# Weight sums and splits of a seven-product pair, emitted in pieces between the running pair's combinations

## The chip, the cores and the metric

One core of a Trainium2 chip runs the whole program in one launch. The metric is the device time of that launch in microseconds (us); less is better. In the profile the engines are PE (TensorE, the matmul engine), PEld (its weight loads), DVE (VectorE), ACT (ScalarE), POOL (GpSimd) and SP (SyncE, which here only issues transfers).

## The reference, cut to what matters

The program computes two layers of a token mixer followed by a gated MLP, in float32. The change is in the MLP of layer 0, which has 512 latent and 256 context tokens (768 columns, kept with paddings as 772), a model width of 1024 and a hidden width of 2816:

```python
u = h @ w_up                                   # 1024 -> 2 x 2816
u = up[:, :-2] * conv_w[0] + up[:, 1:-1] * conv_w[1] + up[:, 2:] * conv_w[2] + conv_b
a, g = jnp.split(u, 2, axis=-1)
return (jax.nn.silu(g) * a) @ w_down
```

## The kernel before

**Three matmuls for one.** An operand is held as a rounded part `h` and a remainder `l = x - h` (a "split": a cast on ACT and a subtraction on DVE). A product is then weight-high by data-high, weight-high by data-low and weight-low by data-high.

**Pairs.** The hidden width is 22 tiles of 128. "Pair j" is tile j of the value half and tile j of the gate half: 256 columns of `w_up`. Pairs 0 to 2 are computed plainly (`up_std`, line 2041). Pairs 3 to 21 use Strassen's scheme with Winograd's sums: the 2x2 blocks are (two halves of the depth) by (value, gate) on the weights, and (two halves of the depth) by (two halves of the 772 columns) on the data. Seven block products take the place of eight. Each is 4 depth tiles x 3 matmuls = 12 matmuls of 386 columns, so a pair is 84 matmuls.

**Weights of a pair** (`job7`, line 1958). Four transfers on SP's queue fill two `raw` tiles. POOL makes four sums of 128x512, q1 to q4 (called S1 to S4 as product operands). ACT and DVE then split the block X11 (from `raw`), the sums, and the second `raw` tile (which holds X12 and X22): five casts and five subtractions. X11 and two of the sums go into four 776-wide slots `ua, ub, la, lb`; the other two sums into `h14, l14`; the second raw tile into `hb, lob`, all 1024 wide. There are 44 slots of the narrow kind (`NSLAB`), of which the split data of the seven products hold 28, and 13 of the wide kind (`N_WIDE`).

**Products and combinations of a pair** (`up7`, line 2062). The four accumulators a0, a1 (value) and g0, g1 (gate) are PSUM banks; odd pairs use `msc` and `dbl0`, even pairs `dbl1` and `sgl` (`sets7`, line 2010), so that two pairs can be under way. In program order: X11 into a0, copied by ACT to t1; S1 into g0, copied by ACT to t5; S2 into a1, added by DVE; an addition on POOL; S3 into g1, added by DVE, and a copy by ACT; X12 into a0; X22 into g0; the gate's additions and its convolution (`conv7`, line 2023: a POOL memset, ACT, and DVE twice or four times); S4 into a1; the value's additions, its convolution, and `gated` (line 2035: SiLU on ACT, a product on POOL, a store).

**What sets the order.** The program emits instructions in an order of its own, and a list scheduler then builds each engine's queue from a simulated timeline: an engine takes the instruction that was emitted first among those whose inputs and slots are ready at that simulated moment. On the chip each queue is worked off in that order, whatever has become ready in the meantime. (In the attention parts PE's order is written by hand; in this stage it is the scheduler's too.) `run_steps` (line 507) emits the weight job of the next pair before the products of the running one (`ahead_by` is 1 here), so all sums and splits of pair j+1 are emitted ahead of every product and combination of pair j. The job of pair 3 is emitted before the first half of plain pair 2.

Of the kernel before, what the change touches and what calls it, by code (L numbers as in the profile page):

```python
# [9 lines left out]
F32R = mybir.dt.float32r  # L10
# [4 lines left out]
ALU = mybir.AluOpType  # L15
# [195 lines left out]
def trunk_kernel(ctx: ExitStack, tc: tile.TileContext, a, out, dbg=None):  # L211
# [3 lines left out]
    V, A, G, SP = (Engine(e, n, est) for e, n in ((nc.vector, "V"), (nc.scalar, "A"), (nc.gpsimd, "G"), (nc.sync, "SP")))  # L215
# [8 lines left out]
    def slab(dt=F32, w=SW, name="sl"):  # L224
        return slabs.tile([128, w], dt, tag="s", name=name)
# [12 lines left out]
    def wide(dt=F32, name="w"):  # L238
        return wides.tile([128, 1024], dt, tag="w", name=name)
# [324 lines left out]
    def rows(w, r0, nk, c0, n):  # L564
        return w[r0:r0 + 128 * nk, c0:c0 + n].rearrange("(k p) n -> p k n", p=128)
# [373 lines left out]
    def layer(l):  # L939
# [792 lines left out]
        tiles = (4, 2, 2, 1)  # L1732
# [152 lines left out]
        def yk(n, k):  # L1885
            hi, lo = s["y"][n][k // 2]
            c = slice(HH * (k % 2), HH * (k % 2) + HH)
            return hi[:, c], lo[:, c]
# [63 lines left out]
        def products7(bank, w, n):  # L1952
            for k in range(4):
                (wh, wl), (yh, yl) = w[k], yk(n, k)
                for i, (w_, m_) in enumerate(((wh, yh), (wh, yl), (wl, yh))):
                    mm(bank, w_, m_, start=k == 0 and i == 0, stop=k == 3 and i == 2)

        def job7(j):

            def load():
                if j == N_STD:
                    for r in (wad, whi, wlo, wst):
                        r.back()
                    tab.clear()
                raw = []
                for half in range(2):
                    t = wide(name="raw")
                    for m, c0 in enumerate((128 * j, FF + 128 * j)):  # L1970
                        SP.dma_start(out=t.rearrange("p (k m n) -> p k m n", k=4, m=2)[:, :, m, :],
                                     in_=rows(w_up, 512 * half, 4, c0, 128))
                    raw.append(t)

                def cut(t):
                    return t.rearrange("p (k n) -> p k n", n=128)

                def tiles(h, l_, c=0, st=128):
                    return [(h[:, c + st * k:c + st * k + 128], l_[:, c + st * k:c + st * k + 128]) for k in range(4)]

                def split(src, h, l_):
                    A.copy(h, src)
                    V.tensor_tensor(l_, src, h.bitcast(F32), op=ALU.subtract)
                xa, xb = (t.rearrange("p (k m n) -> p k m n", k=4, m=2) for t in raw)
                s14, s23 = wide(name="s14"), wide(name="s23")
                q1, q4, q2, q3 = (cut(t[:, c:c + 512]) for t in (s14, s23) for c in (0, 512))

                ua, ub, la, lb = (slab(F32R, name=n) for n in ("ua", "ub", "la", "lb"))
                split(xa[:, :, 0, :], cut(ua[:, 0:512]), cut(la[:, 0:512]))
                G.tensor_tensor(q1, xa[:, :, 1, :], xb[:, :, 1, :], op=ALU.add)  # L1990
                G.tensor_tensor(q2, q1, xa[:, :, 0, :], op=ALU.subtract)
                G.tensor_tensor(q4, xb[:, :, 0, :], q2, op=ALU.subtract)
                G.tensor_tensor(q3, xa[:, :, 0, :], xa[:, :, 1, :], op=ALU.subtract)
                del xa, raw[0]
                h14, l14 = wide(F32R, "h14"), wide(F32R, "l14")
                split(s14[:, :], h14[:, :], l14[:, :])
                hb, lb2 = wide(F32R, "hb"), wide(F32R, "lob")
                split(raw[0][:, :], hb[:, :], lb2[:, :])
                del xb, raw[0]
                split(s23[:, 0:256], ua[:, 512:768], la[:, 512:768])  # L2000
                split(s23[:, 256:1024], ub[:, 0:768], lb[:, 0:768])
                x23 = [(h[:, c:c + 128], l_[:, c:c + 128]) for h, l_, c in
                       [(ua, la, 512), (ua, la, 640)] + [(ub, lb, 128 * k) for k in range(6)]]
                return ({"X11": tiles(ua, la), "X12": tiles(hb, lb2, 0, 256), "X22": tiles(hb, lb2, 128, 256),
                         "S1": tiles(h14, l14), "S4": tiles(h14, l14, 512), "S2": x23[0:4], "S3": x23[4:8]},)
            return load


        sgl2, msc2 = tuple(sgl), tuple(msc)
# [5 lines left out]
        def halves(t, *cols):  # L2015


            if isinstance(t, tuple):
                return [[x[:, 0:HH]] + [u[:, c + HH * i:c + HH * i + HH] for u, c in cols] for i, x in enumerate(t)]
            return [[t.rearrange("p (h n) -> p h n", h=2)[:, :, 0:HH]] +  # L2020
                    [u[:, c:c + HW].rearrange("p (h n) -> p h n", h=2) for u, c in cols]]

        def conv7(m_tile, bank):

            t = slab(name="cv")
            w0, w1, w2 = (cwT[l][:, 44 * i + m_tile:44 * i + m_tile + 1] for i in range(3))
            G.memset(t[:, 0:HW + 2:HW + 1], 0.0)
            for p, x in halves(bank, (t, 1)):
                A.activation(x, p, func=AF.Identity, scale=w1, bias=vecT[l][:, 64 + m_tile:65 + m_tile])
            for c, w in ((2, w0), (0, w2)):  # L2030
                for p, x in halves(bank, (t, c)):
                    V.scalar_tensor_tensor(x, in0=p, scalar=w, in1=x, op0=ALU.mult, op1=ALU.add)
            return t

        def gated(j, ta, tg):
            x = slice(1, 1 + XW)
            s["silu_f"] = A.activation(tg[:, x], tg[:, x], func=AF.Silu)
            G.tensor_tensor(ta[:, x], ta[:, x], tg[:, x], op=ALU.mult)
            G.dma_start(out=adram[j], in_=ta[:, x])

        def up_std(j, half):

            def fn(hi, lo):
                bk = [x for t in sets7[j] for x in banks(t)]
                order = [(k, m) for k in range(4) for m in range(2)] if j + half == 0 else \
                    [(k, m) for m in range(2) for k in range(4)]
                for k, m in order:
                    c = 256 * k + 128 * m
                    ys = [yk(f"Y{half + 1}{g + 1}", k) for g in range(2)]
                    for i, (w_, v) in enumerate(((hi, 0), (hi, 1), (lo, 0))):  # L2050
                        for g in range(2):
                            mm(bk[2 * m + g], w_[:, c:c + 128], ys[g][v], start=half == 0 and k == 0 and i == 0,
                               stop=half == 1 and k == 3 and i == 2)
                    if half == 1 and k == 3:
                        if m == 0:
                            s["ta"] = conv7(j, sets7[j][0])
                        else:
                            gated(j, s.pop("ta"), conv7(KF + j, sets7[j][1]))
                    yield
            return fn  # L2060

        def up7(j):


            def fn(w):
                if j == N_STD:
                    s["y"].pop("Y12")
                bv, bg = sets7[j]
                (a0, a1), (g0, g1) = banks(bv), banks(bg)
                va, vb = slab(name="pa"), slab(name="pb")  # L2070
                t1, t5, t7, u2 = va[:, 0:HH], va[:, HH:HW], vb[:, 0:HH], vb[:, HH:HW]
                products7(a0, w["X11"], "Y11")
                A.copy(t1, a0)
                products7(g0, w["S1"], "T1")
                A.copy(t5, g0)
                products7(a1, w["S2"], "T2")
                V.tensor_tensor(u2, a1, t1, op=ALU.add)
                G.tensor_tensor(t5, t5, u2, op=ALU.add)
                products7(g1, w["S3"], "T3")
                V.tensor_tensor(t7, g1, u2, op=ALU.add)  # L2080
                A.copy(u2, t5)
                products7(a0, w["X12"], "Y21")
                products7(g0, w["X22"], "T4")
                for p, x in halves(bg, (vb, 0)):
                    V.tensor_tensor(p, p, x, op=ALU.add)
                tg = conv7(KF + j, bg)
                products7(a1, w["S4"], "Y22")
                for p, x in halves(bv, (va, 0)):
                    V.tensor_tensor(p, p, x, op=ALU.add)
                gated(j, conv7(j, bv), tg)  # L2090
            return fn
# [246 lines left out]
```

## Time and profile before

| | |
|---|---|
| time, median of 3 runs | 1627.78 us |
| the three runs | 1625.57 to 1628.17 us |
| the profiled execution | 1625.49 us, with a span of 1623.7 us |
| granted TensorE clock, mean of the span | 0.993 |
| busy share of the span | PE 97%, PEld 81%, DVE 65%, ACT 43%, POOL 26% |

The span runs from the first to the last recorded instruction; the 1.8 us outside it are start and end. Times inside are counted from the span's start. Layer 0's seven-product pairs lie at about 455 to 755 us. In a row of a timeline the bracket at the end is the idle time of that engine just before the instruction, and what ended it.

### The profile page before, as it was taken

How to read it: one execution, taken by the hardware profiler on the slowest of the kernel's cores; microseconds unless marked ns; L12 is line 12 of the kernel's file. 1: busy time of each engine (PE TensorE's matmuls, PEld its weight loads, DVE VectorE, ACT ScalarE, POOL GpSimd, SP SyncE). 2: the span in 40 equal slices, each digit the busy share in tenths (PEclk: the TensorE clock that was granted, in tenths of full speed). 3: DMA queues.
4: the chain of work that ended last, by engine and by line, in shares of the span. 5: the costliest groups of instructions: out<-in, count | busy, mean ns of one | idle time of the engine just before them, and what ended most of it. 6: DMA issues, size and time to landing. Idle time of an engine off the chain costs nothing. (4 is left out here: it accounts for less than half of the span.)

```text
span 1623.7 us, 24874 instructions
## 1 busy us (share of the span) xinstructions
PE 1571.5 (97%) x9431; PEld 1317.8 (81%) x9431; DVE 1054.4 (65%) x1860; ACT 706.2 (43%) x1321; POOL 426.1 (26%) x510
## 2 busy tenths in 40 slices
PE   7999999998999999999999999999999999999998
PEld 4777778876999999999888866778776788888886
DVE  6576476875878888887542373957776554545455
ACT  4364354564645544545321242555574432423331
POOL 1105044534356465662000221122202100100000
PEclk9999999999999999999999999999999999999999
DMA  9943342208122323337751555123222233333322
GB/s 317 262 144 117 118 155 71 82 11 246 52 84 84 107 84 96 107 92 237 263 188 52 184 156 134 41 79 120 87 68 88 79 106 98 97 91 91 104 91 78
DMA packets 215411, 193.30 MB, mean 119 GB/s; under 512 B 32648, under 2 KB 185747, under 8 KB 215292
## 3 DMA queue, kind: packets, MB, share of 16 engines
q1 hardware_dynamic: 211036, 174.25, 36.3%
q0 software_dynamic: 4256, 17.47, 2.9%
q8 instruction: 74, 1.21, 0.3%
q14 instruction: 45, 0.37, 0.1%
HBM read 172.51 MB, written 19.18 MB: 118 GB/s over the span
## 5 line engine op out<-in xcount | busy, mean ns | idle before, releaser
L160 ACT CAST whi<-wst 128x1024 fp32r<-128x1024 f32 (+3 forms) x164 | 161.3, 985 | 315.3 <-PE dbl L401 169.3
L160 DVE TENSOR_TENSOR wlo<-wst,whi 128x1024 fp32r<-128x1024 f32 (+1 forms) x139 | 171.5, 1235 | 169.0 <-ACT whi L160 167.3
L160 POOL TENSOR_TENSOR cv<-cv 128x770 f32<-128x770 f32 (+1 forms) x44 | 73.5, 1670 | 382.7 <-ACT cv L160 364.5
L401 PE MATMUL sgl<-hhi,whi 128*128 128x512 f32 (+1 forms) x344 | 132.0, 384 | 2.6 <-ACT cv L160 1.6
L401 PE MATMUL sgl<-hhi,wlo 128*128 128x512 f32 (+1 forms) x344 | 125.8, 366 | 0.0
L401 PE MATMUL sgl<-hlo,whi 128*128 128x512 f32 (+1 forms) x344 | 125.6, 365 | 0.0
L401 PE MATMUL dbl<-alo,whi 128*128 128x512 f32 x346 | 104.9, 358 | 0.0
L401 PE MATMUL dbl<-ahi,whi 128*128 128x512 f32 x346 | 104.9, 358 | 0.0
L401 PE MATMUL dbl<-ahi,wlo 128*128 128x512 f32 x346 | 104.8, 357 | 0.0
L160 DVE SCALAR_TENSOR_TENSOR cv<-dbl,cwT,cv 128x511 f32<-128x511 f32 (+1 forms) x106 | 91.3, 862 | 7.9 <-ACT cv L160 6.8
L401 PE MATMUL dbl<-hhi,wlo 128*128 128x512 f32 x240 | 94.6, 394 | 0.0
L401 PE MATMUL dbl<-hlo,whi 128*128 128x512 f32 x240 | 94.0, 392 | 0.0
L401 PE MATMUL dbl<-hhi,whi 128*128 128x512 f32 x240 | 93.2, 394 | 0.0
L160 DVE SCALAR_TENSOR_TENSOR x<-dbl,modT,x 128x256 f32<-128x256 f32 (+1 forms) x75 | 48.1, 662 | 64.7 <-PE dbl L401 64.2
L160 POOL TENSOR_TENSOR wlo<-wst,whi 128x640 fp32r<-128x640 f32 (+2 forms) x25 | 42.8, 1712 | 157.4 <-ACT whi L160 157.4
L401 PEld LDWEIGHTS sgl<-hhi,whi 128*128 128x128 f32 x344 | 64.8, 188 | 23.0 <-issue 9.1
L401 PEld LDWEIGHTS sgl<-hhi,wlo 128*128 128x128 f32 x344 | 64.8, 188 | 11.3
L401 PEld LDWEIGHTS sgl<-hlo,whi 128*128 128x128 f32 x344 | 64.8, 189 | 10.8 <-issue 0.5
L160 DVE SCALAR_TENSOR_TENSOR x<-sgl,modT,x 128x256 f32<-128x256 f32 (+1 forms) x70 | 44.5, 648 | 44.5 <-PE sgl L401 44.1
L160 POOL TENSOR_TENSOR s<-raw 128x512 f32<-128x512 f32 x38 | 55.1, 1469 | 44.2 <-DMA raw<-in_w_up 38.4
L401 PEld LDWEIGHTS dbl<-ahi,whi 128*128 128x128 f32 x346 | 57.1, 188 | 10.9 <-issue 0.8
L401 PEld LDWEIGHTS dbl<-alo,whi 128*128 128x128 f32 x346 | 57.2, 189 | 10.1
(420 smaller groups left out, 4316.2 us busy)
## 6 DMA issues: line engine op xcount, KB each, us to landing
wst<-in_w_up SPq DMA_DIRECT2D x100, 256.0 KB, 3.2
adaw<-in_w_ada SPq DMA_DIRECT2D x96, 256.0 KB, 5.8
wad<-in_w_ada SPq DMA_DIRECT2D x48, 512.0 KB, 3.8
wst<-in_w_down SPq DMA_DIRECT2D x40, 512.0 KB, 3.5
raw<-in_w_up SPq DMA_DIRECT2D x76, 256.0 KB, 4.3
wst<-in_w_in SPq DMA_DIRECT2D x26, 512.0 KB, 4.0
adram<-cv POOLq DMA_DIRECT2D x22, 385.0 KB, 3.7
af<-adram SPq DMA_DIRECT2D x22, 385.0 KB, 5.4
```

Of the source, the lines that this page charges most:

```text
L160: r = real(*args, **kw)
L401: T.matmul(o, w, m, start=start, stop=stop, **kw)
```

## The change

The sums and splits of the next pair are no longer emitted in one go. `job7` now only allocates and fills the two `raw` tiles, and hands back a generator with the rest; the generator is kept in a list `prep`, and `piece()` runs it to its next `yield`. `up7` calls `piece()` four times, after the copy of t5, after the copy to u2, after the product X12, and after the gate's convolution. `up_std` calls it after every second depth tile, which serves the job of pair 3. The sums are regrouped: q1 and q2 share one wide tile and are split together into `h12, l12`; q3 and q4 share another and are split into the rest of `ua, la` and into `ub, lb`. The number, shapes and engines of all instructions stay as they were. `ua` to `lb` are now read until the last product (S4) and not until the fourth (S3); the 1024-wide pair `h12, l12` is read until the third product, where `h14, l14` was read until the last.

```diff
-                split(xa[:, :, 0, :], cut(ua[:, 0:512]), cut(la[:, 0:512]))
-                G.tensor_tensor(q1, xa[:, :, 1, :], xb[:, :, 1, :], op=ALU.add)
-                G.tensor_tensor(q2, q1, xa[:, :, 0, :], op=ALU.subtract)
-                G.tensor_tensor(q4, xb[:, :, 0, :], q2, op=ALU.subtract)
-                G.tensor_tensor(q3, xa[:, :, 0, :], xa[:, :, 1, :], op=ALU.subtract)
-                h14, l14 = wide(F32R, "h14"), wide(F32R, "l14")
-                split(s14[:, :], h14[:, :], l14[:, :])
-                split(raw[0][:, :], hb[:, :], lb2[:, :])
-                split(s23[:, 0:256], ua[:, 512:768], la[:, 512:768])
-                split(s23[:, 256:1024], ub[:, 0:768], lb[:, 0:768])
...
+                def pieces():
+                    ua, ub, la, lb = (slab(F32R, name=n) for n in ("ua", "ub", "la", "lb"))
+                    s12 = wide(name="s12")
+                    G.tensor_tensor(q1, xa[:, :, 1, :], xb[:, :, 1, :], op=ALU.add)
+                    G.tensor_tensor(q2, q1, xa[:, :, 0, :], op=ALU.subtract)
+                    split(xa[:, :, 0, :], cut(ua[:, 0:512]), cut(la[:, 0:512]))
+                    w["X11"] = tiles(ua, la)
+                    yield
+                    h12, l12 = wide(F32R, "h12"), wide(F32R, "l12")
+                    split(s12[:, :], h12[:, :], l12[:, :])
+                    w["S1"], w["S2"] = tiles(h12, l12), tiles(h12, l12, 512)
+                    yield
+                    s34 = wide(name="s34")
+                    G.tensor_tensor(q3, xa[:, :, 0, :], xa[:, :, 1, :], op=ALU.subtract)
+                    G.tensor_tensor(q4, xb[:, :, 0, :], q2, op=ALU.subtract)
+                    split(s34[:, 0:256], ua[:, 512:768], la[:, 512:768])
+                    split(s34[:, 256:1024], ub[:, 0:768], lb[:, 0:768])
+                    w["S3"], w["S4"] = x34[0:4], x34[4:8]
+                    yield
+                    split(raw[0][:, :], hb[:, :], lb2[:, :])
+                    w["X12"], w["X22"] = tiles(hb, lb2, 0, 256), tiles(hb, lb2, 128, 256)
+                w["pieces"] = pieces()
+                prep.append(w["pieces"])
...
+        def piece():
+            if prep and next(prep[0], prep) is prep:
+                prep.pop(0)
...  up_std
+                    if k % 2:
+                        piece()
...  up7
+                while w["pieces"] in prep:
+                    piece()
                 products7(a0, w["X11"], "Y11")
                 A.copy(t1, a0)
                 products7(g0, w["S1"], "T1")
                 A.copy(t5, g0)
+                piece()
...
                 A.copy(u2, t5)
+                piece()
                 products7(a0, w["X12"], "Y21")
+                piece()
                 products7(g0, w["X22"], "T4")
...
                 tg = conv7(KF + j, bg)
+                piece()
                 products7(a1, w["S4"], "Y22")
```

## Rows read from the trace of the kernel before

**Rows 1.** The page's head and busy shares: engine, busy us (share of span), instructions.
```profile
span 1623.7 us, 24874 instructions
```
**Rows 2.** Busy time by stretch: length, busy us (count) per engine, clock, DMA share, GB/s.
```profile
460.00:745.00 285.00, 280.94 (x1582) 279.12 (x1581) 236.40 (x296) 144.65 (x219) 166.50 (x166) 1.00 0.34 98
...
456.00:468.00 12.00, 11.90 (x59) 11.78 (x59) 11.87 (x16) 8.54 (x12) 6.50 (x9) 0.86 0.10 35
468.00:480.00 12.00, 12.00 (x69) 12.00 (x68) 5.26 (x10) 3.67 (x6) 5.89 (x5) 1.00 0.35 89
...
480.00:600.00 120.00, 118.64 (x667) 117.46 (x667) 99.19 (x123) 61.50 (x94) 67.21 (x69) 1.00 0.33 97
600.00:720.00 120.00, 117.30 (x662) 116.66 (x661) 103.57 (x131) 63.52 (x97) 77.79 (x72) 1.00 0.33 97
```
**Rows 3.** Waits of PE from 440 to 740 us: total us, times, longest us.
```profile
PE msc L401 <- ACT pa L160: 3.0, 2, 2.2
PE msc L401 <- ACT ua L160: 2.5, 1, 2.5
PE sgl L401 <- DVE lb L160: 0.5, 1, 0.5
PE dbl L401 <- ACT pa L160: 0.3, 1, 0.3
```
**Rows 4.** Timeline of POOL, ACT and PE near 592 us: start, us, instruction, idle before.
```profile
589.20 1.29 POOL L160 TENSOR_TENSOR s<-s,raw 128x512 f32<-128x512 f32 x1
...
590.52 0.41 ACT L160 CAST ua<-s 128x256 fp32r<-128x256 f32 x1 [4.42 <-POOL cv L160]
...
592.54 0.48 ACT L160 COPY pa<-msc 128x386 f32<-128x386 f32 x1
...
593.07 0.45 PE L401 MATMUL msc<-hY,hb 128*128 128x386 f32 x1 [0.87 <-ACT pa L160]
```
**Rows 5.** Timeline of POOL, ACT and PE near 652 us.
```profile
647.47 2.98 POOL L160 TENSOR_TENSOR s<-raw 128x512 f32<-128x512 f32 x2
...
650.53 0.67 ACT L160 ACTIVATE cv<-sgl,vecT,cwT 128x386 f32<-128x386 f32 x1 [4.45 <-POOL cv L160]
...
654.96 0.44 PE L401 MATMUL msc<-hY,hb 128*128 128x386 f32 x1 [2.17 <-ACT pa L160]
```
**Rows 6.** Timeline of DVE, ACT and POOL ahead of the first seven-product pair.
```profile
438.81 1.21 DVE L160 TENSOR_TENSOR l<-s,h 128x1024 fp32r<-128x1024 f32 x1
...
440.05 1.05 ACT L160 CAST hb<-raw 128x1024 fp32r<-128x1024 f32 x1 [3.26 <-DVE l L160]
...
445.02 2.88 POOL L160 TENSOR_TENSOR cv<-cv 128x770 f32<-128x770 f32 x1 [7.30 <-ACT cv L160]
...
454.47 0.61 ACT L160 CAST ua<-raw 128x512 fp32r<-128x512 f32 x1
```
**Rows 7.** Sums and splits from 480 to 720 us: count, ns min/median/max, first and last start.
```profile
L160 POOL TENSOR_TENSOR s<-raw x30: 1281/1299/2278, 490.5 to 710.3; 128x512 f32<-128x512 f32 x30
...
L160 DVE TENSOR_TENSOR l<-s,h x16: 1205/1210/1218, 485.7 to 716.7; 128x1024 fp32r<-128x1024 f32 x16
...
L160 DVE TENSOR_TENSOR lob<-raw,hb x16: 1207/1212/2896, 487.7 to 718.7; 128x1024 fp32r<-128x1024 f32 x16
...
L160 DVE TENSOR_TENSOR lb<-s,ub x16: 937/1232/2473, 482.8 to 714.4; 128x768 fp32r<-128x768 f32 x16
```
**Rows 8.** Timeline of PE and ACT from 550 to 579 us: ends of products, start of X11's cast.
```profile
550.59 0.34 PE L401 MATMUL dbl<-lT,ub 128*128 128x386 f32 x1
...
551.62 0.61 ACT L160 CAST ua<-raw 128x512 fp32r<-128x512 f32 x1
...
559.08 0.33 PE L401 MATMUL dbl<-hY,l 128*128 128x386 f32 x1
...
570.22 0.33 PE L401 MATMUL msc<-hY,l 128*128 128x386 f32 x1
...
579.05 0.45 PE L401 MATMUL msc<-hY,ua 128*128 128x386 f32 x1 [0.22 <-DVE cv L160]
```

More of the change, by code (lines that the diff above doesn't have):

```diff
@@ L1966, in load @@
                     tab.clear()
-                raw = []
+                raw, w = [], {}
                 for half in range(2):
@@ L1983, in split @@
                     V.tensor_tensor(l_, src, h.bitcast(F32), op=ALU.subtract)
[L1984 to L1988, printed above, removed]
-                split(xa[:, :, 0, :], cut(ua[:, 0:512]), cut(la[:, 0:512]))
-                G.tensor_tensor(q1, xa[:, :, 1, :], xb[:, :, 1, :], op=ALU.add)
@@ L1991, in load @@
-                G.tensor_tensor(q2, q1, xa[:, :, 0, :], op=ALU.subtract)
-                G.tensor_tensor(q4, xb[:, :, 0, :], q2, op=ALU.subtract)
-                G.tensor_tensor(q3, xa[:, :, 0, :], xa[:, :, 1, :], op=ALU.subtract)
-                del xa, raw[0]
-                h14, l14 = wide(F32R, "h14"), wide(F32R, "l14")
-                split(s14[:, :], h14[:, :], l14[:, :])
-                hb, lb2 = wide(F32R, "hb"), wide(F32R, "lob")
-                split(raw[0][:, :], hb[:, :], lb2[:, :])
@@ L1999, in load @@
-                del xb, raw[0]
-                split(s23[:, 0:256], ua[:, 512:768], la[:, 512:768])
-                split(s23[:, 256:1024], ub[:, 0:768], lb[:, 0:768])
[L2002 to L2005, printed above, removed]
@@ L2006, in job7 @@
-            return load
+                def pieces():
+                    xa, xb = (t.rearrange("p (k m n) -> p k m n", k=4, m=2) for t in raw)
+                    ua, ub, la, lb = (slab(F32R, name=n) for n in ("ua", "ub", "la", "lb"))
+                    s12 = wide(name="s12")
+                    q1, q2 = (cut(s12[:, c:c + 512]) for c in (0, 512))
+                    G.tensor_tensor(q1, xa[:, :, 1, :], xb[:, :, 1, :], op=ALU.add)
[8 more added lines that the diff above has]
+                    s34 = wide(name="s34")
+                    q3, q4 = (cut(s34[:, c:c + 512]) for c in (0, 512))
+                    G.tensor_tensor(q3, xa[:, :, 0, :], xa[:, :, 1, :], op=ALU.subtract)
+                    G.tensor_tensor(q4, xb[:, :, 0, :], q2, op=ALU.subtract)
+                    del xa, raw[0], q1, q2, s12
+                    split(s34[:, 0:256], ua[:, 512:768], la[:, 512:768])
+                    split(s34[:, 256:1024], ub[:, 0:768], lb[:, 0:768])
+                    x34 = [(h[:, c:c + 128], l_[:, c:c + 128]) for h, l_, c in
+                           [(ua, la, 512), (ua, la, 640)] + [(ub, lb, 128 * k) for k in range(6)]]
+                    w["S3"], w["S4"] = x34[0:4], x34[4:8]
+                    yield
+                    hb, lb2 = wide(F32R, "hb"), wide(F32R, "lob")
+                    split(raw[0][:, :], hb[:, :], lb2[:, :])
+                    del xb, raw[0]
+                    w["X12"], w["X22"] = tiles(hb, lb2, 0, 256), tiles(hb, lb2, 128, 256)
@@ L2009, in layer @@
+                w["pieces"] = pieces()
+                prep.append(w["pieces"])
+                return (w,)
+            return load
+        prep = []
+        def piece():
+            if prep and next(prep[0], prep) is prep:
+                prep.pop(0)
         sgl2, msc2 = tuple(sgl), tuple(msc)
```

## The prediction

> **What bounds the kernel now.** I read the page's head first (the span that all shares refer to [rows 1]), then busy time by stretch. From 460 to 745 us, nearly the whole stage that the change touches, PE is busy 280.94 of 285.00 us at granted clock 1.00, DVE 236.40 [rows 2]. The stage is bound by PE, so only PE's idle time can be won here, 4.1 us, and what is lost ahead of it. The waits of PE from 440 to 740 us name it: 3.0 us for ACT's copy to `pa` (t1 or t5, two times), 2.5 us for ACT's cast `ua`, 0.5 us for DVE's `lb`, 0.3 us again for `pa` [rows 3]. The 2.5 us end at the first product of the first pair, at 455 us. Just after it the granted clock of a 12 us stretch is 0.86 and 59 matmuls run in it, against 69 at clock 1.00 in the next [rows 2]: PE had been idle and for a while ran at the lower of its two levels, 1.2 GHz instead of 2.4. Ten matmuls less, at 12.00/69 = 0.174 us each, are 1.7 us. So all that lies there for the change is 3.0 + 0.5 + 0.3 + 2.5 + 1.7 = 8.0 us, 0.5% of the time.
>
> The timelines then show why the copies come late. Near 592 us ACT stands 4.42 us before the cast `ua<-s` of the next pair, whose sum POOL is still making (589.20 + 1.29); the copy `pa<-msc` of the running pair is queued behind and starts at 592.54, and PE has waited 0.87 us at 593.07 [rows 4]. Near 652 us two sums of the next pair (2.98 us) stand on POOL ahead of the memset that the running pair's convolution needs; ACT waits 4.45 us before that convolution, again with the copy behind it, and PE waits 2.17 us [rows 5]. In both places work of the next pair stands ahead of a combination of the running one.
>
> **The change part by part.** Counts, shapes and engines stay: four sums, five casts, five subtractions and four transfers a pair. So nothing is removed or added; all terms are waits.
>
> *Steady stage.* Copies, additions and memsets of the running pair are now emitted before the next pair's sums and casts, and the scheduler takes the earlier emitted when both are ready. The 3.0 and the 0.3 us are waits of just this kind: I take -3.3. Bounds: -3.3, and 0 if the simulated moments leave the same order. The transfers stay where they were in the order (all of `raw` at once, ahead of the pair's products); SP's queue does nothing else here, so its price is 0, hidden under the roughly 15 us of a pair.
>
> *Start.* The job of pair 3 was emitted ahead of plain pair 2, now inside it. Before, its subtraction `l<-s,h` (1.21 us on DVE) and its cast `hb` (1.05 us on ACT) ran at 439 to 441 us, in the time in which POOL stood 7.30 us for the SiLU behind them; the cast `ua` followed only at 454.47 [rows 6]. With these two moved behind, that chain can be up to 1.21 + 1.05 = 2.3 us earlier, but `ua` also needs narrow slots and waits on other work. I take half of the 2.5 us wait and of the 1.7 us of slow clock: -2.1. Bounds: -4.2, and +1.0 if the pieces land later in their new place; that is the length of one cast.
>
> *Price: weights come later.* The four pieces start after the second, fourth, fifth and sixth of seven products, so at about 2/7 to 6/7 of a pair. With a pair of 84 x 0.1775 us = 14.9 us ((118.64 + 117.30)/(667 + 662) per matmul [rows 2]) the last piece starts some 2 us before the pair ends and is needed, as fifth and sixth product of the next, 8.5 us after that. The casts and subtractions of one piece take 2.3 us (1.05 and 1.21), so 8 us are left. Before, one such wait of 0.5 us stands in the trace (`lb`) [rows 3]; I take two or three of that size more, +1.2. Bounds: 0 and 19 x 0.5 = +9.5.
>
> *Slots.* `ua` to `lb` are held longer. In the trace the next cast into them (551.62) follows at once on the last product that reads them (550.59 + 0.34): they already limit. Now the pair would hold them to S4, which ended at 559.4, 8 us later. The wait that this adds is on ACT (the cast), with casts and copies of the running pair behind it. For pairs on the other banks the time is closest: S4 ends at 570.5, the next X11 there begins at 579.05, and itself waited for the bank [rows 8]. 8.5 us less one cast and one subtraction (0.61 and about 1.2 us) leave 6.7 us. I price it at 0 and keep it as a rival. The 1024-wide tiles are freed earlier, which I price at 0: PE has no wait for transfers there [rows 3].
>
> *Sum:* -3.3 - 2.1 + 1.2 = -4.2 us. The profiled execution, 1625.5 us (span 1623.7 [rows 1] and 1.8 us around it), would go to 1621.3. It lies 2.3 us under the median of the runs, 1627.8, which would go to 1623.6.
>
> **A rule that speaks against it.** `l<-s,h` takes 1205 to 1218 ns in all 16 cases, always after the last sum; `lob` and `lb`, which can fall beside sums, reach 2896 and 2473 ns against 1207 and 937 at best [rows 7]. So a subtraction beside a sum can be lengthened by 1.5 to 1.7 us, more than one sum (1.3 us). Now the split of q1 and q2 comes ahead of the sums q3 and q4 and can fall beside them. The Trainium skill, "SBUF — State Buffer", section "Who interferes with whom", states that a VectorE instruction with two SBUF inputs and a GpSimd instruction that reads SBUF exclude each other for the whole instruction. By that rule the later of the two always pays in full; the trace agrees only in part, since the median of `lob` is 1212 ns. What it would make of the time is the third rival.
>
> **The rivals.**
>
> *Nothing is won* (within 3.3 us of before). PE's order is made from simulated times; the three `pa` waits come from the chip's POOL being later than the plan, and such lateness finds another victim. For: the waits are rare, 3 in 19 pairs. Against: both traced cases have work of the next pair in front. Time: 1627.8, chance 0.25.
>
> *All is won.* The start has no wait and no slow clock, and no new wait comes: -8.0, so 1619.8. Against: `ua` at the start waits on more than the moved splits. Chance 0.10.
>
> *Slower by DVE.* DVE is busy (99.19 + 103.57)/16 = 12.7 us a pair [rows 2], 2.2 us under PE's 14.9. If every pair's split of q1 and q2 meets a sum (+1.3 us) and every `lob` its worst (+1.7 us), DVE needs 15.7 us, 0.8 us more than PE: 19 x 0.8 = +15, less the 4 won, 1639. It decides from 2.2 us a pair on; with the mean lengthening of the rows at hand (half a us each) it costs nothing. Chance 0.08.
>
> *Slower by the slots.* If ACT is held more than 6.7 us between S4 and the next X11 of the same banks, PE stands. ACT waits of 4.4 us occur [rows 4, 5], so two in one pair do it. With 1 us in half of the pairs: +9.5 - 4.2 = +5.3, 1633. It decides from 6.7 us on. Chance 0.12.
>
> **How the numbers follow.** The forecast has the remaining 0.45. This kernel's measurement can tell about 0.2%, 3.3 us, from no change. The forecast's own spread is about 2 us, so of its 0.45 some 0.36 is faster and 0.09 within; all of 0.10 for the full gain is faster; of "nothing won" 0.20 is within and 0.05 slower; of the slots 0.09 slower and 0.03 within; all of DVE's 0.08 slower. Faster 0.46, within 0.32, slower 0.22. The range for 8 in 10 runs from just under the full gain, 1618, to just under the slot case, 1632.5; the likeliest case's own is 1621 to 1626.
>
> **What would show it.** Right: between 460 and 745 us PE's idle time falls from 4.1 to 2 us or less, the waits for `pa` are gone, and on ACT no cast of a next pair stands waiting ahead of a copy. The start: the wait for `ua` at the first pair is 1.5 us or less and the stretch after it shows a clock above 0.9. Wrong: waits of PE for `la`, `lb`, `l`, `lob` or the casts add up to more than 3 us; the subtraction of q1 and q2 has a median well over 1.21 us and DVE is busy over 95% of the stage; the casts into `ua` begin more than 7 us after the S4 before; or the time moves outside this stage, of which I have priced nothing.

## The result and the profile after

| | before | after |
|---|---|---|
| median | 1626.67 us | 1641.14 us |
| runs | 1622.53 to 1628.17 (4) | 1640.87 to 1646.21 (4) |
| profiled execution, its span | 1625.49, 1623.7 us | 1640.87, 1638.7 us |

The ratio is 1.0096, with a 95% interval from 1.0078 to 1.0115: slower by 14.5 us. The forecast was 1623.6 us with a range of 1618 to 1632.5, and the time lies above it.

First the stage as a whole, in the view of busy time by stretch of the kernel after (length, busy us and count of PE, PEld, DVE, ACT, POOL, then clock, DMA share, GB/s):

```profile
460.00:745.00 285.00, 274.54 (x1518) 270.55 (x1517) 227.05 (x285) 141.99 (x215) 179.29 (x158) 0.99 0.31 91
584.00:599.00 15.00, 11.62 (x65) 10.96 (x63) 12.84 (x14) 5.67 (x9) 12.55 (x11) 1.00 0.35 110
599.00:603.00 4.00, 3.20 (x10) 3.20 (x11) 2.64 (x5) 3.46 (x7) 2.55 (x3) 0.58 0.01 4
603.00:615.00 12.00, 12.00 (x69) 12.00 (x68) 11.18 (x14) 5.47 (x10) 4.42 (x5) 1.00 0.35 109
```

Against [rows 2] PE has lost 6.4 us of busy time, and 64 matmuls (of 1582) are no longer inside the same 285 us. At 0.1775 us each these are 11.4 us: beside the idle time there is a slower clock (0.58 from 599 to 603 us; see the last section). DVE is not the bound: 227 of 285 us. The waits of PE from 440 to 740 us say where, beside [rows 3]:

```profile
PE msc L401 <- ACT pa L160: 7.0, 4, 3.8
PE sgl L401 <- DVE cv L160: 1.9, 2, 1.1
PE msc L401 <- ACT ua L160: 1.6, 1, 1.6
PE dbl L401 <- DVE pb L160: 1.4, 4, 0.5
PE msc L401 <- DVE la L160: 0.7, 1, 0.7
```

The copy `pa`, whose waits were to go, makes PE wait 7.0 us where it was 3.0. To place the loss I set the start of the k-th matmul of one trace against the k-th of the other. After is 0.7 us ahead at 450 us and 1.4 ahead at 476 us. Then it falls back: by 0.8 us up to 519 us, by 4.8 between 519 and 540, by 4.9 between 584 and 606 (0.9 were won back in between), by 3.5 over the rest of the stage, and by 3.0 from there to 825 us, where it is 14.7 behind (the spans differ by 15.0).

The two big steps are the same event. This is the timeline of the second, on POOL, ACT, DVE and PE (start, length, instruction, and in brackets the idle time before it and its releaser):

```profile
585.64 1.28 POOL L160 TENSOR_TENSOR s<-raw 128x512 f32<-128x512 f32 x1 [7.23 <-DMA raw<-in_w_up]
587.00 1.89 POOL L160 TENSOR_TENSOR s<-s,raw 128x512 f32<-128x512 f32 x1
...
589.91 1.30 POOL L160 TENSOR_TENSOR s<-raw 128x512 f32<-128x512 f32 x1
591.16 2.28 POOL L160 TENSOR_TENSOR s<-raw,s 128x512 f32<-128x512 f32 x1
593.40 1.85 POOL L160 TENSOR_TENSOR cv<-cv 128x770 f32<-128x770 f32 x1
...
588.92 1.05 ACT L160 CAST h<-s 128x1024 fp32r<-128x1024 f32 x1 [4.12 <-POOL s L160]
...
598.53 0.84 ACT L160 ACTIVATE cv<-cv 128x770 f32<-128x770 f32 x1 [4.43 <-DVE cv L160]
599.28 0.46 ACT L160 COPY pa<-msc 128x386 f32<-128x386 f32 x1
...
590.01 2.28 DVE L160 TENSOR_TENSOR l<-s,h 128x1024 fp32r<-128x1024 f32 x1 [1.80 <-ACT h L160]
592.21 1.02 DVE L160 TENSOR_TENSOR sgl<-sgl,pb 128x386 f32<-128x386 f32 x2
593.47 2.85 DVE L160 TENSOR_TENSOR lob<-raw,hb 128x1024 fp32r<-128x1024 f32 x1 [0.24 <-POOL s L160]
596.25 2.19 DVE L160 SCALAR_TENSOR_TENSOR cv<-sgl,cwT,cv 128x386 f32<-128x386 f32 x4
...
599.80 0.69 PE L401 MATMUL msc<-hY,hb 128*128 128x386 f32 x1 [3.77 <-ACT pa L160]
```

Read it backwards from PE. PE waits for the copy `pa` (599.28). The copy stands on ACT behind a SiLU, which waits for the four convolution steps on DVE (596.25). These stand behind the next pair's `lob` (593.47), and `lob` behind POOL's last sum (591.16). The sums stand behind 7.23 us in which POOL waited for a transfer into `raw`. So the work of the next pair is again ahead of the running pair's combination, as in [rows 4, 5], with a late transfer at its head. In the step near 534 us the first sum (519.47) waited 7.51 us for its transfer, and the same row of sums, `lob` and convolution follows.

How often that happens is in the waits of POOL from 460 to 745 us, and what held the transfers is in those of SP's queue. After:

```profile
POOL s L160 <- DMA raw<-in_w_up: 63.9, 13, 8.4
```
```profile
SPq L160 <- DVE lob L160: 116.7, 9, 16.6
SPq L160 <- PE dbl L401: 66.8, 10, 11.7
```

Before, the same two views:

```profile
POOL s L160 <- DMA raw<-in_w_up: 38.4, 7, 8.1
```
```profile
SPq L160 <- PE dbl L401: 129.8, 11, 15.4
SPq L160 <- DVE lb L160: 86.2, 6, 15.6
```

Before, a transfer mostly waited until PE had read a tile to the end, and for a smaller part for `lb`, which was then the last split of a pair; now it mostly waits for `lob`, the last split of a pair in the new order. And that split itself waits: `hb` and `lob` read no sum and nothing of `lb`, so I read the following waits of DVE and ACT in the kernel after as waits for tiles. Neither stands among the waits before:

```profile
DVE lob L160 <- POOL s L160: 16.6, 11, 3.3
```
```profile
ACT hb L160 <- DVE lb L160: 15.4, 8, 4.2
```

The chain that ended last in the stretch from 670 to 712 us shows the loop closed (start, length, what):

```profile
676.09 4.79 DMA raw<-in_w_up
...
681.04 1.29 POOL s L160
...
687.48 3.22 POOL s L160 x2
...
696.19 2.40 PE dbl L401 x12
...
701.22 3.48 POOL s L160 x2
...
704.73 1.24 DVE lob L160
...
707.66 5.01 DMA raw<-in_w_up
```

From transfer to transfer it is 31.6 us for two pairs; PE needs 2 x 14.9 = 29.8 us for them.

### The profile page after: what moved, and what is told of

Its sections match the earlier page's. It is cut to its first block, busy times and chain, and to the rows that moved or that the text cites. A ratio compares the mean times of both kernels' runs of the same rounds, so it can differ in the third digit from the quotient of the medians.

```text
span 1638.7 us, 24904 instructions
## 1 busy us (share of the span) xinstructions
PE 1580.6 (96%) x9431; PEld 1320.4 (81%) x9431; DVE 1051.4 (64%) x1860; ACT 705.8 (43%) x1321; POOL 440.4 (27%) x510
## 3 DMA queue, kind: packets, MB, share of 16 engines
q8 instruction: 74, 1.21, 0.3%
## 4 chain that ended last, share of the span: by engine, by line
PE 70%; DVE 9%; DMA 6%; POOL 6%; ACT 4%; issue 4%; SPq 1%; POOLq 0%; ACTq 0%; DVEq 0%
PE dbl L401 35%; PE sgl L401 24%; PE msc L401 8%; POOL s L160 3%; DMA raw<-in_w_up 3%; PE msc L416 2%; DVE cv L160 1%; DVE la L160 1%; SPq L160 1%; DVE lob L160 1%; POOL cv L160 1%; DMA adaw<-in_w_ada 1%; DMA wst<-in_w_up 1%; ACT cv L160 1%; ACT whi L160 1%
## 5 line engine op out<-in xcount | busy, mean ns | idle before, releaser
L160 POOL TENSOR_TENSOR s<-raw 128x512 f32<-128x512 f32 x38 | 59.9, 1575 | 83.5 <-DMA raw<-in_w_up 67.0
L401 PEld LDWEIGHTS dbl<-ahi,wlo 128*128 128x128 f32 x346 | 57.2, 188 | 10.8 <-DVE wlo L160 0.8
```

Of the source, the lines that this page charges most:

```text
L160: r = real(*args, **kw)
L401: T.matmul(o, w, m, start=start, stop=stop, **kw)
```

## The experiments

Eleven kernels were run against the kernel before, and a twelfth on what they left. "Stage" is from the first to the last of the 1596 matmuls of the seven-product pairs in the trace (before: 301.4 us); "raw" is POOL's wait of sums for transfers, 460 to 745 us (total, times).

| kernel | ratio to before (95%) | stage, us | raw, us |
|---|---|---|---|
| before | 1 | 301.4 | 38.4, 7 |
| after | 1.0096 (1.0078 to 1.0115) | 314.1 | 63.9, 13 |
| e1 new groups, in one go | 1.0160 (1.0131 to 1.0189) | 320.5 | 70.4, 14 |
| e2 old groups, in pieces | 1.0012 (0.9997 to 1.0027) | 297.1 | 23.1, 5 |
| e3 four sums first | 1.0184 (1.0157 to 1.0210) | 321.3 | 83.7, 13 |
| e4 `raw` filled once | 0.9982 (0.9967 to 0.9998) | 294.3 | none |
| e6 S1, S2 in narrow tiles | 0.9998 (0.9985 to 1.0012) | 295.1 | 7.8, 3 |
| e7 before, S1, S4 in narrow tiles | 1.0048 (1.0031 to 1.0064) | 310.6 | 67.5, 15 |
| e8 14 wide, 43 narrow tiles | 1.0127 (1.0110 to 1.0145) | 311.3 | 61.1, 12 |
| e10 12 wide, 45 narrow tiles | 1.0211 (1.0193 to 1.0230) | 331.0 | 70.9, 10 |
| e11 S4 right after S3 | 1.0211 (1.0183 to 1.0238) | 325.2 | 91.9, 14 |
| e12 `hb`, `lob` split late | 1.0013 (0.9997 to 1.0028) | 296.1 | 32.8, 10 |
| e13 e6, first pair in one go | 1.0001 (0.9987 to 1.0015) | 295.0 | 14.9, 3 |
| e14 tiny q3, q4 | 1.0043 (1.0020 to 1.0066) | 302.8 | 75.0, 12 |

**Is it the pieces or the grouping?** e1 keeps the new groups and runs all pieces at once:

```diff
                 w["pieces"] = pieces()
-                prep.append(w["pieces"])
+                for _ in w["pieces"]:
+                    pass
```

> The new grouping of sums (q1 with q2, q3 with q4) kept, but all sums and splits emitted in one go ahead of the running pair, as before. Theory A (the raw tiles are now given back only by the last piece, so the next transfer and the sums that wait for it come late, and they stand at the head of POOL's queue): the pieces alone cost the time, so this goes back to 1625 to 1631 us. Theory B (the narrow slots are held to S4 by the new grouping): the grouping alone costs it, so this stays at 1637 us or more. Theory C (the split of q1 and q2 falls beside the sums q3 and q4 and is lengthened on DVE): that order is kept here, so it stays at 1634 us or more and the subtraction l keeps a median near 1.8 us.

1650.35 us, slower still than after. e2 keeps the pieces and goes back to the old groups (q1, q4 in one wide tile and split into `h14, l14`; q2, q3 in the other and split into the narrow tiles):

```diff
-                    s12 = wide(name="s12")
...
+                    s14, s23 = wide(name="s14"), wide(name="s23")
...
-                    w["S3"], w["S4"] = x34[0:4], x34[4:8]
+                    w["S2"], w["S3"] = x23[0:4], x23[4:8]
```

> The old grouping (q1 with q4 in the 1024-wide pair, q2 with q3 in the narrow slots, which are free again after S3), emitted in four pieces at the same four places. Theory A: the pieces are there, so it stays at 1636 us or more. Theory B: the narrow slots come free early again, so it goes back to 1625 to 1631 us. Theory C: one of the two later sums now comes ahead of the wide split, so about half of the 14 us goes, 1632 to 1636 us.

1629.0 us, no different from before. So the pieces by themselves cost nothing; with the new groups they even save 9 us (1650.35 against 1641.14). What costs is the new grouping, some 24 us in one go; it changes the order of the sums and their storage together.

**The lengthened split.** e3 makes all four sums in the first piece, so that the split of q1 and q2 should no longer meet the sums q3 and q4:

```diff
+                    s34 = wide(name="s34")
...
+                    G.tensor_tensor(q3, xa[:, :, 0, :], xa[:, :, 1, :], op=ALU.subtract)
+                    G.tensor_tensor(q4, xb[:, :, 0, :], q2, op=ALU.subtract)
                     split(xa[:, :, 0, :], cut(ua[:, 0:512]), cut(la[:, 0:512]))
...
                     w["X11"] = tiles(ua, la)
                     yield
```

> The changed kernel with all four sums in the first piece, ahead of the split of q1 and q2; one of the two raw tiles comes free earlier, the other still in the last piece. Theory A: little changes, 1635 us or more, perhaps a few us from the one tile. Theory B: no change, 1639 to 1643 us. Theory C: the subtraction l goes back to 1.21 us and the time to 1626 to 1632 us.

1654.61 us. It did not do what I wanted: the median of `l<-s,h` rose to 2.35 us (1.79 after, 1.21 before). In its trace 11 of the 18 subtractions `l` from 460 to 745 us were lengthened beside the running pair's product `cv<-cv` on POOL, which the edit leaves alone, and only 5 beside a sum. So it neither clears nor convicts the lengthening.

**The transfers.** e4 fills the two `raw` tiles once, for the first pair, and uses them for all, so that the other 18 pairs compute with the first pair's weights:

```diff
-                    t = wide(name="raw")
+                    if j == N_STD:
+                        t = wide(name="raw")
...
-                    raw.append(t)
+                        once.append(t)
+                    raw.append(once[half])
```

> The changed kernel with the raw tiles filled once, for pair 3, and used for all 19 pairs: it leaves out the transfers of the other 18 pairs, and their weights. No sum waits for a transfer any more. Theory A: 1620 to 1629 us, POOL's idle time before sums for transfers gone. Theory B: no change but for some us, 1637 us or more. Theory C: no change, 1637 us or more.

1623.11 us, the stage 19.8 us shorter than after: without a late transfer there is no loss. It also takes away every other effect of the `raw` tiles (two of 13 wide tiles are held for good, none is allotted anew), so it names the loop and not the link in it that is too long.

**Which tiles are held?** e6 exchanges the storage of the changed kernel: S1 and S2 go with X11 into `ua` to `lb`, S3 and S4 into a 1024-wide pair. Order of sums, splits and pieces stay.

```diff
-                    h12, l12 = wide(F32R, "h12"), wide(F32R, "l12")
-                    split(s12[:, :], h12[:, :], l12[:, :])
...
+                    split(s12[:, 0:256], ua[:, 512:768], la[:, 512:768])
+                    split(s12[:, 256:1024], ub[:, 0:768], lb[:, 0:768])
...
+                    h34, l34 = wide(F32R, "h34"), wide(F32R, "l34")
+                    split(s34[:, :], h34[:, :], l34[:, :])
```

> The changed kernel with the storage of the two sum pairs exchanged: S1 and S2 are split into the narrow slots beside X11, S3 and S4 into the 1024-wide pair; same four pieces, same order of sums and splits. The narrow slots are free after the third product, the wide pair is held to S4. Theory B (the narrow slots are short, and the new grouping holds them to S4): back to 1622 to 1631 us. Theory W (the wide tiles are short; the next transfer waits for one): more wide tiles are held than in the changed kernel, so 1641 us or more. Theory O (only the order of sums and splits within the job matters): no change, 1638 to 1645 us.

1625.77 us: the whole loss is gone, with the new order. e7 does the opposite to the kernel before: S1 and S4 into the narrow tiles (then read until the last product), S2 and S3 into the wide pair.

```diff
-                split(s14[:, :], h14[:, :], l14[:, :])
+                split(s14[:, 0:256], ua[:, 512:768], la[:, 512:768])
+                split(s14[:, 256:1024], ub[:, 0:768], lb[:, 0:768])
```

> The kernel before with its storage exchanged: S1 and S4 are split into the narrow slots, so these are held to S4, S2 and S3 into the 1024-wide pair, free after the fourth product; all in one go, old order of the sums. Theory B: slower by 8 to 25 us, 1634 us or more. Theory W: no slower, 1622 to 1628 us. Theory O: the order of sums is the old one, so 1624 to 1630 us.

1633.0 us, and the sums now wait 67.5 us for `raw`. So storage matters in either order of the sums, though the loss in e7 (7 us) is half of the one after. e8 and e10 trade one tile of one kind for one of the other in the changed kernel (constants `N_WIDE`, `NSLAB`):

```diff
-NSLAB = 44
+NSLAB = 43
...
-N_WIDE = 13
+N_WIDE = 14
```

> The changed kernel with 14 wide tiles and 43 narrow slots in place of 13 and 44. Theory B: one narrow slot less makes it slower, 1645 us or more. Theory W: the transfers no longer wait, 1626 to 1634 us. Theory O: no change, 1639 to 1643 us.

```diff
-NSLAB = 44
+NSLAB = 45
...
-N_WIDE = 13
+N_WIDE = 12
```

> The changed kernel with 12 wide tiles and 45 narrow slots in place of 13 and 44. Theory B: one narrow slot more helps, 1628 to 1637 us. Theory W: one wide tile less makes it slower, 1646 us or more. Theory O: no change, 1639 to 1643 us.

With 12 wide tiles the stage is 16.9 us longer than after, though there is a narrow tile more; with 14 only 2.8 us shorter, and its stage begins 9.1 us later than after (460.8 against 451.7 us). The times are 1661.43 and 1647.09 us. One wide tile less hurts, one more (with a narrow one less) does not cure.

At this point every slow kernel held S4 in narrow tiles and every fast one did not (but for e4, which has no transfers), which fits both "narrow tiles are held too long" and "wide tiles are short". e11 and e12 part the two. e11 shortens the hold of the narrow tiles by two products:

```diff
                 products7(g1, w["S3"], "T3")
...
+                products7(a1, w["S4"], "Y22")
                 products7(a0, w["X12"], "Y21")
...
-                products7(a1, w["S4"], "Y22")
```

> The changed kernel with one line moved: the product S4 follows S3 directly (order X11, S1, S2, S3, S4, X12, X22), so that ua to lb are read until the fifth product and not until the seventh; storage, pieces and their places stay. Theory N (the narrow slots held until the last product keep the next cast into ua, and with it the whole chain of splits, late): the hold is two products, 4.2 us, shorter; the time falls to 1626 to 1631 us, VectorE's l and lob follow their casts earlier, and the waits of the sums for raw fall from 64 us in 13 to under 35 us. Theory W (the stock of 1024-wide tiles is what is short, from the last piece's hb and lob waiting long for their product): hb is needed 2 us later than in the changed kernel, so its stock lies longer; no gain, 1640 to 1645 us. Theory G (it is the order of sums and splits of the new grouping, wherever it is stored): no change, 1641 us.

1658.57 us: theory N is wrong, and W's "no gain" was too mild. e12 leaves that hold alone and emits the last piece in the pair's own turn:

```diff
-                while w["pieces"] in prep:
+                while "S4" not in w:
                     piece()
...
                 A.copy(t5, g0)
+                if w["pieces"] in prep:
+                    piece()
                 piece()
...
                 tg = conv7(KF + j, bg)
-                piece()
```

> The changed kernel with its last piece (the split of the second raw tile into hb and lob) moved out of the pair before: it is emitted in the pair's own turn, after the copy of t5, that is three products before X12 wants it; the other three pieces keep their places. Theory W (hb and lob stand ready too long, and fill the 1024-wide tiles): the lifetime of hb and lob falls from some 33 us to under 20, the wide tiles are all full much less than 29% of the stage; the time falls to 1625 to 1632 us. Theory N (narrow slots held to the last product): nothing changes for ua to lb, 1638 to 1645 us. Theory R (what counts is when the second raw tile is given back): it is given back some 5 us later in the order, so the sums wait longer for raw, over 70 us, and the time goes up to 1645 to 1655 us.

1625.83 us, as W had it: R and N fall. The views that were bad are good again. PE from 460 to 745 us, the only wait of PE that the view lists there, and the two waits of DVE and POOL:

```profile
460.00:745.00 285.00, 284.10 (x1602) 283.00 (x1601) 242.88 (x304) 151.94 (x229) 184.82 (x166) 1.00 0.33 102
```
```profile
PE dbl L401 <- DVE pb L160: 0.9, 2, 0.7
```
```profile
DVE lob L160 <- ACT hb L160: 2.2, 4, 1.2
```
```profile
POOL s L160 <- DMA raw<-in_w_up: 32.8, 10, 5.0
```

`lob` no longer waits for a sum and `hb` no longer for `lb`. But W's own sign did not come. I worked out each tile's life, from first write to last read, by matching the order of the queues with the instructions of the trace: `hb` lives 27.0 us before, 33.4 after, 25.5 in e6, 35.6 in e11 and 29.6 in e12, not under 20; and all 13 wide tiles are in use for 0.6% of the time before, 29% after, 15.8% in e11 and 46% in e12. So "how full" does not tell slow from fast. Nor does it tell them apart that a transfer waits for a split; in e12 nearly all do:

```profile
SPq L160 <- DVE lb L160: 141.5, 15, 15.3
SPq L160 <- DVE l L160: 59.1, 10, 10.1
```

There the transfers wait for splits that come earlier in the order than `lob`, and the sums' longest wait is 5.0 us, not 8.4. What e12 shows is that moving the last piece alone takes the loss away.

e13 is e6 with the first pair's job in one go:

```diff
                 w["pieces"] = pieces()
-                prep.append(w["pieces"])
+                if j == N_STD:
+                    for _ in w["pieces"]:
+                        pass
+                else:
+                    prep.append(w["pieces"])
```

> The changed kernel with the storage exchanged (sums q1, q2 split into the narrow slots with X11, sums q3, q4 into a 1024-wide pair; that alone took 1625.8 us), and the job of the first seven-product pair emitted in one go as in the kernel before; all later pairs in four pieces. If the some 3.7 us that the exchanged kernel loses at the start of the stage come from the first pair's pieces between the steps of the plain pair: 1622 to 1624 us, PE's wait for ua at the first product not above 2.5 us. If they come from the storage: 1625 to 1627 us.

1626.37 us, and the first product begins at 457.8 us (458.8 in e6, 455.1 before). So at most 1 us of the late start comes from the first pair's pieces. The rest goes with the exchanged storage, which e7 has too (458.3 us); the wait behind it was not traced. No version that computes the whole result beats the kernel before.

**Length or lateness?** e14 keeps tiles and transfers, and makes q3 and q4 short (it leaves all but 8 of every 128 columns of S3 and S4 out of the result):

```diff
-                    G.tensor_tensor(q3, xa[:, :, 0, :], xa[:, :, 1, :], op=ALU.subtract)
-                    G.tensor_tensor(q4, xb[:, :, 0, :], q2, op=ALU.subtract)
+                    G.memset(s34[:, :], 0.0)
+                    G.tensor_tensor(q3[:, :, 0:8], xa[:, :, 0, 0:8], xa[:, :, 1, 0:8], op=ALU.subtract)
+                    G.tensor_tensor(q4[:, :, 0:8], xb[:, :, 0, 0:8], q2[:, :, 0:8], op=ALU.subtract)
```

> The changed kernel with the sums q3 and q4 cut to 8 of every 128 columns (the rest of their tile is set to zero, so S3 and S4 are mostly left out of the result); tiles, splits, transfers and pieces stay. A memset reads nothing and the two sums that are left read a sixteenth, so the splits of q1 and q2 and of the second raw tile no longer stand beside long reads of POOL. Theory C (what costs is that subtractions on VectorE and sums on POOL lengthen each other): the median of l falls from 1.79 to about 1.22 us and the longest lob from 2.86 to under 1.5, and the time falls to 1625 to 1631 us. Theory T (what costs is the loop by which a raw tile is given back by the last split and the next transfer starts late; the lengthening is only part of it): the splits are short, but the sums still wait over 45 us for raw in the stage and the time stays at 1634 to 1641 us. Between 1631 and 1634: both, in about equal parts.

1633.46 us, in the band "both". Its trace is more telling than its time:

```profile
460.00:745.00 285.00, 282.33 (x1575) 280.97 (x1575) 230.03 (x298) 145.47 (x220) 151.72 (x183) 0.99 0.33 99
```
```profile
POOL s L160 <- DMA raw<-in_w_up: 75.0, 12, 8.0
```
```profile
L160 DVE TENSOR_TENSOR lob<-raw,hb x18: 1203/1222/1258, 470.5 to 725.8; 128x1024 fp32r<-128x1024 f32 x18
```
```profile
PE sgl L401 <- ACT ahi L160: 3.3, 2, 2.3
```

The sums wait as long for `raw` as in the slow kernels, yet PE is busy 282.33 us and, matmul by matmul, within about 1 us of before or ahead of it (0.8 behind at 476 and at 745 us, 2.7 ahead at 680). `lob` is short (min, median, max in ns). `l` stayed at a median of 1.77 us, which C did not expect, but it does not speak against the lengthening: 13 of its 18 cases began beside the running pair's products and additions on POOL (`cv<-cv`, `pa<-pa,pb`), which e14 leaves as they are. With only a memset beside its start, `l` took 1.22 to 1.23 us (at 482.35, 598.46, 628.80 and 659.51).

So late transfers by themselves need not cost PE anything. I take it that they cost when what is queued behind them, the sums and the splits, is too long to fit before the running pair's combination. That is argued from this one kernel, in which the scheduler's order can have moved too. Some 7 us that this kernel still loses come after 745 us, where its largest wait is for `ahi` (the last row, 740 to 840 us).

## Why the prediction was wrong, point by point

**The step that failed is "Slots", in its last sentence**: "The 1024-wide tiles are freed earlier, which I price at 0: PE has no wait for transfers there". I followed one pair of them, `h12, l12`, and left out the others; and that PE does not wait for a transfer does not say that POOL, whose queue holds PE's combinations, does not. The last piece's tiles (`hb` 27.0 to 33.4 us, `lob` 24.5 to 30.3), the second sum tile (`s23` 7.3, `s34` 15.5) and `raw` (16.9 to 19.4 in the mean of its two tiles) are all held longer. The steady stage's "The transfers stay where they were in the order", with its price of 0, fell with it: a transfer's place in the order stayed, but it also needs a tile, and that is now mostly given back by the pair's last split. The sums' waits for `raw` went from 38.4 to 63.9 us, and the stage is 314.1 - 301.4 = 12.7 us longer. Both edits that take this away without undoing the pieces and the new order of sums (e6, e12) bring the time back to that of before.

**The rival "Slower by the slots"** had the sign and the kind of resource and the wrong tiles. It held the narrow tiles to S4; e11 shortens that hold and is slower, e12 keeps it and is fast. My claim that the narrow tiles "already limit" rested on one coincidence in time.

**Steady stage, -3.3.** Wrong in this kernel: PE waits 7.0 us for `pa`, four times, not 0. Right in the mechanism where the loop is out of the way: in e2, e6 and e12 no wait for `pa` is listed from 460 to 745 us, and between 476 and 745 us PE wins 2.0, 4.8 and 3.7 us on the kernel before.

**What I did not price at all: after the stage.** The prediction names this gap in its last paragraph. These gains do not outlast the next step. e12 is 3.8 us ahead at 747 us and 0.9 behind at 825, with PE waiting

```profile
PE sgl L401 <- ACT ahi L160: 2.7, 1, 2.7
```

for the down projection's first data, which goes through DRAM; before has no such wait. That names 2.7 of the 4.7 us; the rest I did not find. So even without the loop the time is that of before (1625.8 us in e6 and e12), inside the range but without the forecast gain.

**Start, -2.1.** Right in sign: the wait for `ua` is 1.6 us against 2.5 [rows 3], and after is 1.4 us ahead of before at 476 us, 0.7 of it already at 450, ahead of the stage. The slow clock stayed: from 456 to 468 us it is 0.86 as before.

**Weights later, +1.2.** About right taken by itself: PE's waits for weights that a split had not finished are 0.7 us (`la`), beside those for `ua` at the start; the others of that list are combinations.

**Slower by DVE.** DVE did not become the bound, so the rival fails as I put it. But the lengthening is real, and I had its partner wrong. The longest `lob` of [rows 7] (2896 ns) lay beside the running pair's product on POOL, not beside a sum. Before:

```profile
673.55 1.84 POOL L160 TENSOR_TENSOR cv<-cv 128x770 f32<-128x770 f32 x1 [4.17 <-ACT cv L160]
...
673.58 2.90 DVE L160 TENSOR_TENSOR lob<-raw,hb 128x1024 fp32r<-128x1024 f32 x1
```

So "more than one sum" needs no more than one partner. After:

```profile
L160 DVE TENSOR_TENSOR l<-s,h x18: 1217/1788/2694, 463.0 to 731.7; 128x1024 fp32r<-128x1024 f32 x18
```

The median was 1.21 us. Of these 18, 11 were lengthened by that product, which had begun ahead of them (one of them below), 2 by an addition of the running pair, and 2, at the two big steps, by a sum:

```profile
619.17 1.87 POOL L160 TENSOR_TENSOR cv<-cv 128x770 f32<-128x770 f32 x1
...
620.33 1.79 DVE L160 TENSOR_TENSOR l<-s,h 128x1024 fp32r<-128x1024 f32 x1 [1.35 <-ACT h L160]
```

In the chain at 599 us the last sum (2.28, beside `l`, usually 1.3) and `lob` (2.85, beside the product `cv<-cv`, usually 1.2) are 2.6 us longer than usual, most of PE's 3.8 us. I let it count only if DVE became full; it also counts where such a row of work stands ahead of a copy that PE needs.

**What stays open.** Which link of the loop is the deciding one: e6 and e12 change tiles and queue order together, since the scheduler's simulated moments move with each. That 14 wide tiles don't cure it (e8) is not explained. A rival is left as well: the medians of `l` and `lob` together are 2.6 us or less in every kernel that is not slower (2.4 before, 2.5 in e12) and 3.0 or more in every slower one. No run changes the product on POOL that lengthens most of them, so whether this is a part of the cause or follows from the order is not shown.

## What to carry to other kernels

When an edit regroups buffers, list every tile of the pool with its first write and last read before and after, and not only the one that the edit shortens; then ask who gives back the tile into which the next transfer goes, and how late. A gain in one stage is only a gain if the first wait of the next stage is not already fixed by something else. And when work of the next iteration waits at the head of an in-order queue, look at the length of what is queued, not only at the wait: in e14, with the sums shortened, 75.0 us of such waits cost PE next to nothing inside the stage.

## What the runs showed of the hardware

*Subtractions on VectorE and POOL's sums and products take turns.* `l` at 523.84 us lay beside a sum that ran from 523.74 to 525.04, and took 2.27 us: up to 525.04 and then another 1.07, little under its usual 1.2. The sum started at 525.00, beside it, also took 2.27 instead of 1.28. One that began first kept its time (`l` at 494.75: 1.23 us, with the next sum beside it for 1.12 us, and that sum took 2.28). The rule in the Trainium skill, "SBUF — State Buffer", "Who interferes with whom", is borne out here: one of the two waits for the other's end. Mostly it is the one recorded as later; but three times before, `lb` began 0.32 to 0.34 us ahead of a sum and yet paid (at 558.71 it took 2.46 us, the sum 1.31). The prediction's "agrees only in part" came from medians of a kernel in which the two seldom met.

*Similar idle time, with and without a fall of the clock.* After PE's 2.17 us wait at 654.96 us in the kernel before [rows 5] the next matmuls soon started 0.177 us apart, at the full 2.4 GHz (granted clock 1.00). In the kernel after PE waited 0.76 us ahead of 531.89 and 1.94 us ahead of 534.60, and then 11 matmuls ran at 1.2 GHz (0.50):

```profile
532.00:535.00 3.00, 1.06 (x5) 0.74 (x6) 1.94 (x3) 2.64 (x5) 0.94 (x1) 0.97 0.00 0
535.00:538.00 3.00, 3.00 (x11) 3.00 (x10) 3.00 (x6) 2.54 (x5) 1.09 (x1) 0.50 0.00 0
```

At 0.32 us from start to start in place of 0.177 that adds 1.6 us to a wait of 1.9. After the 3.77 us wait that ended at 599.80 some ten more ran so.
